# A hybrid attention and mLSTM trunk: the mixer's transposes move from TensorE to transposing DMAs, all but two, and the second token tile's output takes its mLSTM half first

## The chip, the cores and the metric

The kernel runs on one core of a Trainium2 chip. The metric is the device time of one execution in microseconds (us). The time before the change is the median of three runs, 963.02 us (962.27 to 963.16).

## The reference

The input x has 256 tokens of 1024 channels (batch 1). There are two layers. Each adds to x a half-step SwiGLU network, a mixer, and another half-step SwiGLU network; every branch has an RMS norm ahead of it and one behind it. The mixer, cut to what matters:

```python
proj = h @ w_in                                  # 1024 -> 3080 columns
da_q, da_k, da_v, ml_qk, ml_v, ml_o, ml_g = split(proj)
# differential attention, 4 heads of 2 x 64, causal in chunks of 64 tokens
q = rope(da_q) * 64 ** -0.5; k = rope(da_k)
p = softmax(where(mask, q @ k.T, -inf))          # two maps per head
y_da = rmsnorm((p[0] - lam * p[1]) @ v) * (1 - lam_init)
# mLSTM, 4 heads, chunked recurrence over the tokens
q, k = split(silu(causal_conv(ml_qk)))           # 4 taps over the tokens
y_ml = sigmoid(ml_o) * rmsnorm(numerator / denominator)
out = concat([y_da, y_ml]) @ w_out               # 1024 -> 1024
```

Everything is in 32-bit floats.

## The kernel before

The 256 tokens are two tiles of 128 tokens, numbered 0 and 1 here and in the code (`t`). Weights are streamed from memory in pieces of 1 MB (`wr`), by SyncE's DMA queue and into three buffers. ScalarE rounds each half piece to the reduced 32-bit format (`wh`, L288), VectorE takes the difference (`wl`, L289), and TensorE multiplies in three passes: activation high by weight high, high by low, low by high (`mm3`, L401, L402, L403). In the three passes the activation is the stationary side and 512 weight columns move.

A layer is a list of such products. In the mixer, `traverse` lays out the products of the six projections in 56 or so steps, one step being the three passes for 128 input channels of one token tile. The order of projections is: the mLSTM's q and k (whose convolution follows), the attention's Q and K with rope, the mLSTM's values, the attention's values, and the mLSTM's output gate. All other work of the mixer (gates, convolution, scores, softmax, numerators) is cut into stages, which `stages` lists; the table `AT` (L40) says ahead of which step each stage is written. So TensorE's stream alternates projection steps with short groups of the stages' own products. Which instruction goes when on each engine is decided by the scheduler of the framework, which keeps the written order on TensorE nearly as it is and may move instructions on the others; `high_priority` blocks pull an evacuation forward. Every engine then runs its own list in order.

PSUM has two banks for projections (tag `pin`), two for transposes (`ptr`) and four for the rest (`bk`). A projection's bank is free again once its evacuation has read it: `nat` for the convolution input (`conv_input`), `rv` for Q and K (`rope`), `vx` and `vd` for the values, `so` (a Tanh) for the output gate. With two banks, a projection waits for the evacuation of the one but last.

The places where the mixer turns a 128x512 tile of tokens by channels into channels by tokens are these, each by four TensorE transposes into one `ptr` bank and one ScalarE copy out of it:

- the convolution input `nat`, both tiles (`conv_input_t`, L898), into the padded buffer `xpad`;
- the rope's result `ra`, Q and K for both tiles (`roped`, L1067), into `qkT`;
- the combined attention weights `p`, once for tile 0 and twice for tile 1 (`combine`, L1110), into `aT`; here VectorE first forms p[0] + c * p[1] in place (L1122);
- the attention output `y` and the gated mLSTM output `so` of both tiles (`attended`, `outputs_ml`), followed by `hilo`, which scales them and splits them into a high and a low part (L884, L885).

The feed-forward networks already turn their hidden activations in another way (`ffn_planes`, L530). ScalarE copies the tile, read as 16-bit words, into two planes of low and high halves (L535); a transposing DMA on SyncE's queue turns the planes (L537); VectorE joins the halves to 32-bit words again (L539).

At the end of a mixer, `outp(t, part, hf)` multiplies one half of the output vector (`part` 0 is attention, 1 is mLSTM) of tile `t` into 512 output columns `hf`, four steps of three passes each.

## Time and profile before

| | before |
|---|---|
| median of three runs | 963.02 us (962.27 to 963.16) |
| the profiled execution | 962.02 us |
| its span in the trace | 960.2 us |
| granted TensorE clock | 0.999 |
| busy: TensorE matmul, its weight load | 952.8 us, 788.9 us |
| busy: VectorE, ScalarE, GpSimd | 638.7 us, 571.2 us, 29.5 us |
| DMA traffic | 189.32 MB, mean 197 GB/s |

The profile is of one execution. Its own time of 962.02 us is 1.0 us below the median of the runs; the span is the part that the trace covers, from the first recorded instruction to the last. PE is TensorE's matmul stream and PEld its weight load, which overlaps it; DVE is VectorE, ACT ScalarE, POOL GpSimd, and SP is SyncE, whose queue issues nearly all DMAs. L numbers are lines of the kernel before. The two mixers lie at about 191 to 290 us and 664 to 763 us of the span; the feed-forward networks fill the rest.

### The profile page before, as it was taken

Reading aid. Unit: us, or ns where it says so; the run is one execution under the profiler, and the core shown is the slowest. Engines: PE = TensorE matmul, PEld = TensorE weight load, DVE = VectorE, ACT = ScalarE, POOL = GpSimd, SP = SyncE. Lnnn points to the kernel's source line nnn. Section 1 sums busy time; section 2 is a strip of 40 time slices with the busy share of each in tenths; the row PEclk is TensorE's granted clock in tenths of the full one; section 3 lists DMA queues with packets and bytes.
Section 4 is the critical chain, followed back from the end, with each engine's and each line's share of the span. In section 5 each row is a group of like instructions: output and inputs, shape, how many; then the busy total and the mean of one; then the engine's idle time right before and its main releaser. Section 6 shows DMA issues by size and latency. Waiting matters only on the chain.

```text
span 960.2 us, 12037 instructions
## 1 busy us (share of the span) xinstructions
PE 952.8 (99%) x4523; PEld 788.9 (82%) x4523; DVE 638.7 (67%) x945; ACT 571.2 (59%) x937; POOL 29.5 (3%) x55
## 2 busy tenths in 40 slices
PE   9999999999999999999999999999999999999997
PEld 7888888888888888888888888888888888888885
DVE  6765655689867766555687555566988676755553
ACT  8755554577856655454476555555778466555542
POOL 2000000000010000000000000000001000000000
PEclk9999999999999999999999999999999999999999
DMA  8996656236352975676458666653454257765621
GB/s 317 328 288 202 225 193 219 105 132 241 116 192 91 299 245 193 218 247 176 154 189 283 206 225 208 196 187 128 172 202 174 90 182 256 272 205 192 225 72 44
DMA packets 69879, 189.32 MB, mean 197 GB/s; under 512 B 45274, under 2 KB 46426, under 8 KB 49086
## 3 DMA queue, kind: packets, MB, share of 16 engines
q1 hardware_dynamic: 69246, 187.95, 58.0%
q8 instruction: 35, 0.57, 0.2%
q10 hardware_dynamic: 576, 0.61, 0.2%
q14 instruction: 22, 0.18, 0.1%
HBM read 177.01 MB, written 1.05 MB: 185 GB/s over the span
## 4 chain that ended last, share of the span: by engine, by line
PE 97%; DVE 1%; DMA 1%; ACT 0%; issue 0%; POOLq 0%; DVEq 0%; ACTq 0%
PE pin L401 13%; PE pin L402 13%; PE pin L403 13%; PE bk L401 10%; PE bk L402 10%; PE bk L403 10%; PE ptr L402 6%; PE ptr L403 6%; PE ptr L401 6%; PE pin L610 1%; PE ptr L610 1%; PE ptr L879 1%; PE ptr L427 1%; DMA wr<-in_w_dram 1%; PE bk L1094 1%; PE ptr L615 1%
## 5 line engine op out<-in xcount | busy, mean ns | idle before, releaser
L289 DVE TENSOR_TENSOR wl<-wr,wh 128x1024 fp32r<-128x1024 f32 x324 | 389.2, 1221 | 180.4 <-ACT wh L288 174.4
L288 ACT ACTIVATE wh<-wr 128x1024 fp32r<-128x1024 f32 x324 | 333.9, 1055 | 171.2 <-DMA wr<-in_w_dram 44.1
L401 PE MATMUL pin<-wh,both 128*128 128x512 f32 x560 | 221.2, 396 | 0.0
L403 PE MATMUL pin<-wh,both 128*128 128x512 f32 x560 | 218.3, 390 | 0.0
L402 PE MATMUL pin<-wl,both 128*128 128x512 f32 x560 | 218.2, 390 | 0.0
L401 PE MATMUL bk<-wh,hh 128*128 128x512 f32 x352 | 137.4, 390 | 0.1
L402 PE MATMUL bk<-wl,hh 128*128 128x512 f32 x352 | 137.0, 389 | 0.0
L403 PE MATMUL bk<-wh,hl 128*128 128x512 f32 x352 | 136.9, 389 | 0.0
L403 PEld LDWEIGHTS pin<-wh,both 128*128 128x128 f32 x560 | 105.1, 188 | 22.3
L401 PEld LDWEIGHTS pin<-wh,both 128*128 128x128 f32 x560 | 105.3, 188 | 22.0 <-issue 0.7
L402 PEld LDWEIGHTS pin<-wl,both 128*128 128x128 f32 x560 | 105.3, 188 | 20.6
L403 PE MATMUL ptr<-wh,both 128*128 128x512 f32 x256 | 99.4, 389 | 0.0
L402 PE MATMUL ptr<-wl,both 128*128 128x512 f32 x256 | 99.4, 389 | 0.0
L401 PE MATMUL ptr<-wh,both 128*128 128x512 f32 x256 | 98.9, 389 | 0.0
L401 PEld LDWEIGHTS bk<-wh,hh 128*128 128x128 f32 x352 | 66.1, 188 | 14.0 <-ACT hh L550 0.5
L403 PEld LDWEIGHTS bk<-wh,hl 128*128 128x128 f32 x352 | 66.1, 188 | 13.7
L402 PEld LDWEIGHTS bk<-wl,hh 128*128 128x128 f32 x352 | 66.1, 188 | 13.5
L539 DVE COPY hT<-turned 128x1024 uint16<-128x1024 uint16 x40 | 30.3, 757 | 41.9 <-DMA turned<-planes 41.5
L401 PEld LDWEIGHTS ptr<-wh,both 128*128 128x128 f32 x256 | 48.1, 188 | 10.0
L402 PEld LDWEIGHTS ptr<-wl,both 128*128 128x128 f32 x256 | 48.1, 188 | 10.0
L550 ACT ACTIVATE hh<-hT 128x256 fp32r<-128x256 f32 x80 | 28.9, 409 | 46.0 <-DVE hT L539 46.0
L403 PEld LDWEIGHTS ptr<-wh,both 128*128 128x128 f32 x256 | 48.1, 188 | 9.9
(210 smaller groups left out, 891.9 us busy)
## 6 DMA issues: line engine op xcount, KB each, us to landing
wr<-in_w_dram SPq DMA_DIRECT2D x162, 1024.0 KB, 5.2
gpost<-in_gpost_dram SPq DMA_DIRECT2D x6, 512.0 KB, 6.3
wr<-in_w_dram SPq DMA_DIRECT2D x2, 512.0 KB, 6.1
wr<-in_w_dram SPq DMA_DIRECT2D x3, 256.0 KB, 4.3
x<-in_x_dram SPq DMA_DIRECT2D x3, 256.0 KB, 4.4
turned<-planes SPq DMA_TRANSPOSE x40, 4.4
out_dram<-x SPq DMA_DIRECT2D x2, 256.0 KB, 2.1
x<-in_x_dram SPq DMA_DIRECT2D x2, 128.0 KB, 3.0
```

Of the source, the lines that this page charges most:

```text
L288: ia = nc.scalar.activation(hi, raw[:, j], AF.Copy)
L289: iv = nc.vector.tensor_tensor(lo, raw[:, j], hi.bitcast(F32), op=ALU.subtract)
L401: mm(ps, xh, wh, start=start, stop=False)
L402: mm(ps, xh, wl, start=False, stop=False)
L403: mm(ps, xl, wh, start=False, stop=stop)
L427: nc.tensor.transpose(ptr[:, k, :], x[:, (4 * hf + k) * P:(4 * hf + k + 1) * P], self.ident)
L539: nc.vector.tensor_copy(hT.rearrange("p b n -> p (b n)").bitcast(U16).rearrange("p (n u) -> p u n", u=2), turned.rearrange("p (u b) n -> p ...
L550: self.nc.scalar.activation(hh, h, AF.Copy)
L610: self.nc.tensor.matmul(b, self.cols(w[kh], k)[0][:, c], both[kh][:, k].rearrange("p i t -> p (i t)"), start=kh == 0 and k == 0, stop=Fals ...
L615: self.nc.tensor.matmul(b[:, 0:NT * P], self.cols(w[kh], k)[1][:, c], both[kh][:, k, 0:NT].rearrange("p i t -> p (i t)"), start=False, sto ...
L879: self.T(ptr[:, b, :], a[:, b * P:(b + 1) * P], self.tr.ident)
L1094: self.mm(pcs[c][:, h, :], self.qkT[0][rows, h0 + h, t * P:(t + 1) * P], self.qkT[1][rows, h0 + h, 0:nk], start=True, stop=True)
```

## The change

The mixer's turns go the way of the feed-forward networks' hidden activations: planes on ScalarE, a transposing DMA on SyncE's queue, a joining copy on VectorE. Only `y` and `so` of tile 0 keep TensorE's transposes. Per mixer that is eleven groups of four transposes gone from TensorE, and eleven times planes, DMA and joining copy added. Nine of ScalarE's evacuations go with them; for `y` and `so` of tile 1 `hilo` stays and reads the joined tile. The issue of the DMA moves to where the tile is made (`turn` in `conv_input`, `rope`, `combine`, `attend`, `output_gate`), and the joining copy stands where the transposes were; for the attention weights that is a stage of its own (`weights`). The factor 1/8 of Q goes into the scale of its evacuation (`rhalf`). `combine` writes its sums into a tile of its own, `pc`. The two stages `attended` are written earlier or outside `stages`, the table `AT` has a value for every new stage, and the output projection of tile 1 takes `part` 1 first.

```diff
+    def turn(self, v):
+        planes = self.t2("planes", (P, 2, 512), U16)
+        self.nc.scalar.activation(planes, v.bitcast(U16).rearrange("p (n u) -> p u n", u=2), AF.Copy)
+        turned = self.t2("turned", (P, 8, P), U16)
+        self.nc.sync.dma_start_transpose(turned, planes.rearrange("p u n -> p (u n)"))
+        return turned
+
+    def joined(self, out, turned):
+        self.nc.vector.tensor_copy(out.bitcast(U16).rearrange("p b (n u) -> p u b n", u=2),
+                                   turned.rearrange("p (u b c) n -> p u b (c n)", u=2, b=out.shape[1]))
...
         outp(0, 1, 0)
         m.outputs_ml(1)
+        m.attended(1)
         outp(0, 1, 1)
         yield "done", po[0], gpost
+        outp(1, 1, 0)
+        outp(1, 1, 1)
+        yield "next"
         outp(1, 0, 0)
         outp(1, 0, 1)
-        yield "next"
-        outp(1, 1, 0)
-        outp(1, 1, 1)
         yield "done", po[1], gpost
...
-        self.nat = nat
+        self.nat.append(tr.turn(nat))
 
     def conv_input_t(self, t):
-        self.act(self.xpad[:, :, 3 + t * P:3 + (t + 1) * P], self.transposed(self.nat), AF.Copy)
+        self.tr.joined(self.xpad[:, :, 3 + t * P:3 + (t + 1) * P], self.nat[t])
...
-        self.rot.append(a)
+        self.rot.append(tr.turn(a))
...
-        self.act(self.qkT[i][:, :, t * P:(t + 1) * P], self.transposed(self.rot[2 * i + t]), AF.Copy, scale=scale)
+        self.tr.joined(self.qkT[i][:, :, t * P:(t + 1) * P], self.rot[2 * i + t])
...
-        ptr = tr.bank_tr((P, t + 1, nh, P))
+        pc = tr.t2("pc", (P, t + 1, nh, P))
         for h in range(nh):
-            p = self.p[t, h0][h]
-            self.stt(p[:, 0, :], p[:, 1, :], c1[:, h:h + 1], p[:, 0, :], op0=ALU.mult, op1=ALU.add)
-            for kt in range(t + 1):
-                self.T(ptr[:, kt, h, :], p[:, 0, kt * P:(kt + 1) * P], tr.ident)
-        self.act(aT[:, :, hs, :], ptr, AF.Copy)
+            p = self.p[t, h0][h].rearrange("p c (a b) -> p c a b", b=P)
+            self.stt(pc[:, :, h, :], p[:, 1], c1[:, h:h + 1], p[:, 0], op0=ALU.mult, op1=ALU.add)
+        self.flat[t, h0] = aT[:, :, hs, :], tr.turn(pc.rearrange("p a h b -> p (a h b)"))
+
+    def weights(self, t, h0):
+        out, turned = self.flat[t, h0]
+        self.tr.joined(out.rearrange("p a h b -> p a (h b)"), turned)
...
-        self.y[t] = y
+        y = y.rearrange("p h e -> p (h e)")
+        self.y[t] = tr.turn(y) if t else y
...
-        y = self.transposed(self.y[t].rearrange("p h e -> p (h e)"))
+        y = self.whole(self.y[t]) if t else self.transposed(self.y[t])
...
-        self.so.append(so)
+        so = so.rearrange("p h e -> p (h e)")
+        self.so.append(tr.turn(so) if t else so)
```

The scheduler's order shows three places in the first mixer. In these rows line numbers are those of the kernel listed; in the kernel after the change, planes are L544, the joining copy L550, the rope's evacuation `rv` L1071 and the gate's exponentials still L266.

VectorE, at the start of the mixer, before: `gs` to `lg` are the gate's small steps, `g_591` holds the gate rows that TensorE transposes next, and `wl` are weight splits.

```order
L433 TENSOR_TENSOR both_1700<-xg_1829,both_1700 128x4x128
L289 TENSOR_TENSOR wl_0_1863<-wr_1861,wh_0_1864 128x1024
L289 TENSOR_TENSOR wl_1_1867<-wr_1861,wh_1_1868 128x1024
L940 TENSOR_REDUCE gs_1896<-bk_1895 128x16
...
L949 SCALAR_TENSOR_TENSOR lg_1917<-gn_1897 128x8
L755 TENSOR_SCALAR c_neglam<-c_neglam 128x1
L289 TENSOR_TENSOR wl_0_1982<-wr_1980,wh_0_1983 128x1024
L957 SCALAR_TENSOR_TENSOR g_591<-gn_1897,lg_1917 128x4x4 x2
L289 TENSOR_TENSOR wl_1_1992<-wr_1980,wh_1_1993 128x1024
L973 SCALAR_TENSOR_TENSOR gt_2011<-c_scan,bk_1931 100x256
```

The same place after; `xpad` is the padded convolution input of tile 0.

```order
L433 TENSOR_TENSOR both_1700<-xg_1833,both_1700 128x4x128
L550 COPY xpad<-turned_1817 128x2x4x128
L289 TENSOR_TENSOR wl_0_1861<-wr_1859,wh_0_1862 128x1024
L289 TENSOR_TENSOR wl_1_1865<-wr_1859,wh_1_1866 128x1024
L950 TENSOR_REDUCE gs_1894<-bk_1893 128x16
...
L959 SCALAR_TENSOR_TENSOR lg_1915<-gn_1895 128x8
L289 TENSOR_TENSOR wl_0_1991<-wr_1989,wh_0_1992 128x1024
L289 TENSOR_TENSOR wl_1_2001<-wr_1989,wh_1_2002 128x1024
L967 SCALAR_TENSOR_TENSOR g_591<-gn_1895,lg_1915 128x4x4 x2
L983 SCALAR_TENSOR_TENSOR gt_2026<-c_scan,bk_1929 100x256
```

The joining copy into `xpad` now stands ahead of the splits `wl_0_1861` and `wl_1_1865`, and both splits of the next piece stand ahead of the gate rows, where one did.

ScalarE, around Q's tile 1, before: `rv_1996` is the evacuation of Q's tile 1 from bank `pin_1961`, `eE` are the gate's two exponentials, `conv` the first tap of the convolution in four blocks.

```order
L288 ACTIVATE wh_1_2132<-wr_2113 128x1024
L1057 ACTIVATE rv_1996<-pin_1961,rs_204_1840 128x512
L288 ACTIVATE wh_0_2182<-wr_2179 128x1024
L899 ACTIVATE xpad<-ptr_2032 128x4x128
L266 ACTIVATE eE_2050<-bk_2047 128x512
L907 ACTIVATE conv_2038<-xpad,c_568 128x256 x4
L266 ACTIVATE eE_2055<-bk_2052 128x512
L260 ACT_TABLE_LOAD
L1071 ACTIVATE qkT_2057<-ptr_2058 128x4x128
```

The same place after; `planes_1966` is for the rope's result of Q's tile 0, and `rv_2005` is the evacuation of Q's tile 1.

```order
L288 ACTIVATE wh_0_2190<-wr_2187 128x1024
L917 ACTIVATE conv_2048<-xpad,c_568 128x256 x4
L544 ACTIVATE planes_1966<-ra_1957 128x1024
L266 ACTIVATE eE_2060<-bk_2057 128x512
L266 ACTIVATE eE_2065<-bk_2062 128x512
L260 ACT_TABLE_LOAD
L1071 ACTIVATE rv_2005<-pin_1970,rhalf_2008 128x512
```

Q's evacuation went from ahead of the convolution, the exponentials and the table load to behind all of them. On TensorE the second exponential's input `bk_2062` is made directly ahead of `pin_2067`, K's tile 1, which takes the bank of `pin_1970`:

```order
L1008 MATMUL bk_2057<-md,ul 128x512
L1009 MATMUL bk_2057<-c_mask,c_identr 128x512
L1008 MATMUL bk_2062<-md,ul 128x512
L1009 MATMUL bk_2062<-c_mask,c_identr 128x512
L401 MATMUL pin_2067<-wh_0_1992,both_1690 128x512
L402 MATMUL pin_2067<-wl_0_1991,both_1690 128x512
```

Before, two groups of transposes stood around these four products; no other product moved there.

VectorE, around the attention weights, before: `p` are the softmax maps of tile 0 being combined, `bk_2357` and the next are the scores of tile 1, whose masked part is set (L1097) and whose maxima are then taken (L1098, `mx`).

```order
L1122 SCALAR_TENSOR_TENSOR p_2272<-p_2272,c_262_2338 128x128 x2
L1122 SCALAR_TENSOR_TENSOR p_2273<-p_2273,c_262_2338 128x128 x2
L289 TENSOR_TENSOR wl_1_2558<-wr_2500,wh_1_2559 128x1024
L289 TENSOR_TENSOR wl_0_2644<-wr_2642,wh_0_2645 128x1024
L1097 MEMSET bk_2357 64x2x64
L1098 TENSOR_REDUCE mx_2355<-bk_2357 128x2
L1097 MEMSET bk_2358 64x2x64
L1098 TENSOR_REDUCE mx_2355<-bk_2358 128x2
```

The same place after; `turned_2346` comes from the transposing DMA of tile 0's combined weights `pc_2339`.

```order
L1136 SCALAR_TENSOR_TENSOR pc_2339<-p_2275,c_270_2336 128x128 x2
L1136 SCALAR_TENSOR_TENSOR pc_2339<-p_2276,c_270_2336 128x128 x2
L289 TENSOR_TENSOR wl_1_2529<-wr_2496,wh_1_2530 128x1024
L289 TENSOR_TENSOR wl_0_2643<-wr_2641,wh_0_2644 128x1024
L1111 MEMSET bk_2354 64x2x64
L1111 MEMSET bk_2355 64x2x64
L550 COPY aT_259_2258<-turned_2346 128x2x512
L1112 TENSOR_REDUCE mx_2352<-bk_2354 128x2
```

The joining copy of tile 0's weights now stands between the masks and the maxima of tile 1.

More of the change, by code (lines that the diff above doesn't have):

```diff
@@ L39 @@
 AHEAD = 2
-AT = (0, 2, 6, 6, 7, 22, 24, 24, 24, 24, 36, 40, 24, 46, 34, 50, 43, 52, 52, 57, 61, 60, 61, 67, 67, 69, 71, 78, 74, 74, 78, 84)
+AT = (0, 2, 6, 6, 7, 10, 22, 24, 24, 24, 24, 36, 40, 28, 46, 34, 50, 46, 52, 52, 57, 61, 60, 61, 67, 67, 69, 71, 78, 72, 74, 78, 80, 82, 83)
 FIRST = """W6 V3 T000 T001 A000 A001 B000 B001 W1 V1 T002 T003 H00 L00 A002 A003 B002 B003 W1 V1 M000 H01 L01
@@ L148 @@
     TAGS = {"kwn": ("kwn", 1), "aT0": ("aT0", 1), "aT1": ("aT1", 1)}
-    for _n in ("nat", "ra", "rb", "rv", "tmp", "y", "so", "xg", "h", "planes", "turned", "hT"):
+    for _n in ("nat", "ra", "rb", "rv", "tmp", "y", "so", "xg", "h", "planes", "turned", "hT", "pc"):
         TAGS[_n] = ("ev", 5)
@@ L530, in ffn_planes @@
     def ffn_planes(self, h):
-        nc = self.nc
-        planes = self.t2("planes", (P, 2, 512), U16)
-        nc.scalar.activation(planes, h.rearrange("p t j -> p (t j)").bitcast(U16).rearrange("p (n u) -> p u n", u=2), AF.Copy)
-        turned = self.t2("turned", (P, 8, P), U16)
-        nc.sync.dma_start_transpose(turned, planes.rearrange("p u n -> p (u n)"))
         hT = self.t2("hT", (P, 4, P))
-        nc.vector.tensor_copy(hT.rearrange("p b n -> p (b n)").bitcast(U16).rearrange("p (n u) -> p u n", u=2),
-                              turned.rearrange("p (u b) n -> p u (b n)", u=2))
+        self.joined(hT, self.turn(h.rearrange("p t j -> p (t j)")))
         ops = [self.ffn_operand() for _ in range(NT)]
@@ L731, in outp @@
                 self.mm3(po[t][hf], yh[:, k, :], yl[:, k, :], *self.cols(ws[2 * part + k // 2], 2 * (k % 2) + hf),
-                         start=part == 0 and k == 0, stop=part == 1 and k == 3)
+                         start=part == t and k == 0, stop=part != t and k == 3)
         outp(0, 0, 0)
@@ L765, in __init__ @@
         self.conved = None
-        self.rot, self.qkT, self.so, self.p = [], [], [], {}
+        self.nat, self.rot, self.qkT, self.so, self.p, self.flat = [], [], [], [], {}, {}
         self.aT, self.lsum, self.hn, self.y = [None] * NT, [None] * NT, [None] * NT, [None] * NT
@@ L836, in stages @@
             self.gate_rows,
+            lambda: self.conv_input_t(0),
             self.gate_chain,
@@ L843, in stages @@
             lambda: self.conv((0, 1)),
-            lambda: self.roped(0, 0, 0.125),
+            lambda: self.roped(0, 0),
             self.conv_silu,
-            lambda: self.roped(0, 1, 0.125),
+            lambda: self.roped(0, 1),
             self.weighted_qk,
-            lambda: self.roped(1, 0, 1.0),
+            lambda: self.roped(1, 0),
             lambda: self.scores(0, 0),
             self.intra_weights,
-            lambda: self.roped(1, 1, 1.0),
+            lambda: self.roped(1, 1),
             lambda: self.scores(1, 0),
@@ L859, in stages @@
             lambda: self.normed_ml(1),
+            lambda: self.weights(0, 0),
             lambda: self.attend(0),
+            lambda: self.attended(0),
+            lambda: self.weights(1, 0),
+            lambda: self.weights(1, 2),
             lambda: self.attend(1),
-            lambda: self.attended(0),
-            lambda: self.attended(1),
         ))
@@ L1055, in rope @@
         v8, a8, b8 = (i.rearrange("p (g d) -> p g d", g=8) for i in (v, a, b))
+        scale = self.r[t]
+        if len(self.rot) < NT:
+            scale = tr.small("rhalf", (P, 1))
+            self.ts(scale, self.r[t], 0.125, None, op0=ALU.mult)
         with tr.tc.high_priority():
-            self.rv = self.act(v, pin, AF.Copy, scale=self.r[t])
+            self.rv = self.act(v, pin, AF.Copy, scale=scale)
             i = tt(a8, v8, tr.rope[:, 0, t, :].unsqueeze(1).broadcast_to([P, 8, 64]), op=ALU.mult)
@@ L1064, in rope, with roped @@
             self.turned = tt(a, a, b, op=ALU.add)
-        self.rot.append(a)
-    def roped(self, i, t, scale):
+        self.rot.append(tr.turn(a))
+    def roped(self, i, t):
         if t == 0:
             self.qkT.append(self.tr.t4("qkT", (P, 4, S)))
-        self.act(self.qkT[i][:, :, t * P:(t + 1) * P], self.transposed(self.rot[2 * i + t]), AF.Copy, scale=scale)
+        self.tr.joined(self.qkT[i][:, :, t * P:(t + 1) * P], self.rot[2 * i + t])
     def values_da(self, pin, t):
@@ L1142, in attend, with whole @@
         self.tt(y, po, sc.unsqueeze(2).broadcast_to([P, 4, P]), op=ALU.mult)
-        self.y[t] = y
+        y = y.rearrange("p h e -> p (h e)")
+        self.y[t] = tr.turn(y) if t else y
+    def whole(self, turned):
+        out = self.tr.t2("hT", (P, 4, P))
+        self.tr.joined(out, turned)
+        return out
     def attended(self, t):
-        y = self.transposed(self.y[t].rearrange("p h e -> p (h e)"))
+        y = self.whole(self.y[t]) if t else self.transposed(self.y[t])
         self.yT[t][0] = self.hilo(y, self.tr.gda[:, self.l:self.l + 1], 0, t)
@@ L1213, in outputs_ml @@
     def outputs_ml(self, t):
-        y = self.transposed(self.so[t].rearrange("p h e -> p (h e)"))
+        y = self.whole(self.so[t]) if t else self.transposed(self.so[t])
         self.yT[t][1] = self.hilo(y, self.tr.gml[:, self.l:self.l + 1], 1, t)
```

1 line of the change is left out of this document (removed).

## The prediction

> **What bounds the kernel now.** I read the page first: the busy shares, then the chain that ended last.
>
> ```profile
> PE 952.8 (99%) x4523; PEld 788.9 (82%) x4523; DVE 638.7 (67%) x945; ACT 571.2 (59%) x937; POOL 29.5 (3%) x55
> PE 97%; DVE 1%; DMA 1%; ACT 0%; issue 0%; POOLq 0%; DVEq 0%; ACTq 0%
> ```
>
> TensorE is busy all the time and the chain runs on it. So a TensorE instruction that disappears is worth its full time, and any wait that makes TensorE stand still costs its full time. Other engines cost nothing until TensorE needs something from them. The averages hide the stage that the change touches, so next I read windows over the two mixers, and one inside the first.
>
> ```profile
> 191.00:286.00 95.00, 95.00 (x535) 78.61 (x534) 78.42 (x151) 69.75 (x152) 6.22 (x9) 1.00 0.47 172
> 664.00:759.00 95.00, 95.00 (x535) 78.65 (x534) 78.27 (x148) 70.02 (x152) 7.33 (x9) 1.00 0.47 172
> 220.00:225.00 5.00, 5.00 (x24) 4.14 (x23) 5.00 (x12) 4.97 (x8) 0.00 (x0) 1.00 0.77 299
> ```
>
> The columns after the length are busy time of PE, PEld, DVE, ACT and POOL, the granted clock, the DMA share and GB/s. The mixers are alike, so one is worked out and doubled. In a mixer VectorE is busy for 78.4 of 95 us (67% over the whole span) and in 220 to 225 us both VectorE and ScalarE are full. What the change hands to them lands where they have least to spare.
>
> **What is removed.** On the chain of waits the groups of four transposes stand as follows (start, us):
>
> ```profile
> 217.62 0.44 PE ptr L879 x4
> 248.23 0.62 PE ptr L1124 x4
> 256.38 0.58 PE ptr L1124 x4
> 260.65 0.44 PE ptr L1124 x4
> ```
>
> Per mixer the code drops eleven groups: two of the convolution input, four after the rope, three of the attention weights, one each of the token-1 halves y and so. Eight at 0.44 and 0.62 + 0.58 + 0.44 make 5.16 us; for two mixers 10.3 us. All of it is on the path, so that is the most that the change can gain. The scheduled order shows that TensorE's other work stays the same, but for the attention product of token 1, which moves 24 rows later.
>
> **What is added.** Per mixer eleven plane copies on ScalarE, eleven transposing DMAs in SyncE's queue, eleven joining copies on VectorE. The FFN already does all three, so their prices stand in the trace:
>
> ```profile
> L535 ACT ACTIVATE planes<-h 128x1024 uint16<-128x1024 uint16 x40 | 42.1, 1052 | 8.6 <-DVE h L528 8.4
> L539 DVE COPY hT<-turned 128x1024 uint16<-128x1024 uint16 x40 | 30.3, 757 | 41.9 <-DMA turned<-planes 41.5
> L1125 ACT ACTIVATE aT<-ptr 128x512 f32<-128x512 f32 x6 | 3.5, 589 | 0.0
> DMA to landing us min/median/max: 2.7/4.4/8.9
> ```
>
> A turn by TensorE costs 0.44 us and an evacuation of 0.59 on ScalarE. By DMA it costs 1.05 + 2.7 (the fastest; 4.4 is the median) + 0.76 = 4.5 us at least, passed through three queues. VectorE gets 11 x 0.76 = 8.3 us more per mixer, ScalarE 11 x 1.05 less nine evacuations of 0.6, so 6.2 us. VectorE then has 86.7 us of work in about 90: nearly full, not yet the bound. What suffers first could be the weight halves (L289). One that by the order is first read by K's products for token 0:
>
> ```profile
> 203.36 1.22 DVE L289 TENSOR_TENSOR wl<-wr,wh 128x1024 fp32r<-128x1024 f32 x1 [0.24 <-ACT wh L288]
> 214.72 0.39 PE L401 MATMUL pin<-wh,both 128*128 128x512 f32 x1
> ```
>
> It is done at 204.6 and read at 214.7: 10 us ahead. The 8.3 us come spread over the mixer, and TensorE's own delay gives the splits as much time again, so I cost the splits at nothing; with that cover gone it is the third rival.
>
> The Trainium skill, VectorE: DVE Perf Modes, section Rules for kernel authors, advises TensorE for a 128x128 transpose if PSUM can be the target, which speaks against this change; its section on the three transpose paths prices the DMA's at 1309 ns for one block of 16-bit values. By that figure the eight blocks of one plane tile would take 10.5 us (an estimate), and the sum below would grow by up to 4 x 7.8 us a mixer; the trace has 2.7 us, which I use.
>
> **Gate rows.** A joining copy for the convolution input now stands on VectorE ahead of two pairs of weight splits, and the gate's rows (before at 204.50) behind both pairs.
>
> ```profile
> 194.05 12.20 SPq L282 DMA_DIRECT2D wr<-in_w_dram  x3
> 198.85 2.36 DVE L289 TENSOR_TENSOR wl<-wr,wh 128x1024 fp32r<-128x1024 f32 x2 [0.25 <-ACT wh L288]
> 204.50 0.25 DVE L957 SCALAR_TENSOR_TENSOR g<-gn,lg 128x16 f32<-128x16 f32 x2
> 205.39 0.60 PE L967 MATMUL bk<-c,g 128*100 128x128 f32 x4
> ```
>
> The turn is queued behind the weight load of 194.05; I put its landing at 199.75. Copy 0.76, two splits 2.36, small steps 1.0, two splits 2.36: the rows come at about 206.3. TensorE is there 0.36 earlier than before, at 204.8. Stall about 1.45 us, from 0 (an earlier landing, splits in between) to 3 (landing at the 4.4 median).
>
> **Rope of Q's second token.** Before, the evacuation rv ran as soon as its products were done. Now it is last on ScalarE behind four convolution steps, a plane copy, both gate exponentials and the table load. The next projection reuses the PSUM bank that rv empties, so TensorE waits for rv.
>
> ```profile
> 214.92 0.69 ACT L1057 ACTIVATE rv<-pin,rs 128x512 f32<-128x512 f32 x1 [0.30 <-PE pin L403]
> 219.06 2.07 ACT L907 ACTIVATE conv<-xpad,c 128x256 f32<-128x256 f32 x4
> 221.03 0.58 ACT L266 ACTIVATE eE<-bk 128x512 f32<-128x512 f32 x1
> 221.63 1.28 ACT L260 ACT_TABLE_LOAD   x1
> 218.59 0.40 PE L999 MATMUL bk<-c_mask,c_identr 128*128 128x512 f32 x1
> 219.18 0.48 PE L401 MATMUL pin<-wh,both 128*128 128x512 f32 x1
> ```
>
> The second exponential reads the product that TensorE makes directly before the blocked projection, so part of this wait can't be hidden whatever the load: 0.4 (product) + 0.58 + 1.28 + 0.69 = 2.85 us after removing what overlaps. By the queue I get more, since the convolution steps wait for VectorE's second copy into the padded input, and VectorE is full here:
>
> ```profile
> 210.00:215.00 5.00, 5.00 (x24) 4.14 (x23) 4.82 (x11) 3.83 (x7) 0.00 (x0) 1.00 0.02 7
> 215.00:220.00 5.00, 5.00 (x28) 4.17 (x27) 4.94 (x7) 3.48 (x6) 0.00 (x0) 1.00 0.59 225
> ```
>
> With the gate work 1.45 later in that queue I put the copy's end at 217.75; convolution to 219.8, planes 220.8, two exponentials 221.9, table 223.2, rv 223.9. TensorE, 1.45 late and 1.24 early, would come at about 219.5. Stall 4.4 us (2.85 to 5.5, a copy 1 us later). To here, 5.85 of stalls less 1.24 of transposes: +4.6.
>
> The Trainium skill, ScalarE: Activation LUTs, section What ACT_TABLE_LOAD costs, adds a drain of about 1380 ns to the load's 1283. The trace shows the load at 1.28 us and the next instruction starting at its end; by the page this stall would be 1.4 us longer.
>
> **K's second token to the first scores.** The same rv step, one token later, waits behind one plane copy: a stall of 1.0, less two groups of 0.44: +0.1 (-0.9 to +1.5).
>
> **Scores to the last projection.** Here a whole chain becomes serial: token 0's exponentials, combination, planes, DMA, joining copy, which stands ahead of token 1's maxima on VectorE; these release token 1's exponentials, and behind them stands the evacuation vd that frees the next projection's bank.
>
> ```profile
> 239.98 1.16 PE L1094 MATMUL bk<-qkT,qkT 64*128 64x128 f32 x16
> 246.34 0.40 ACT L266 ACTIVATE p<-bk,mx 128x128 f32<-128x128 f32 x1
> 247.32 1.14 DVE L1122 SCALAR_TENSOR_TENSOR p<-p,c 128x128 f32<-128x128 f32 x4
> 250.95 0.69 DVE L1098 TENSOR_REDUCE mx<-bk 128x2 f32<-128x512 f32 x1
> 251.73 0.47 ACT L266 ACTIVATE p<-bk,mx 128x256 f32<-128x256 f32 x1 [1.87 <-DVE mx L1098]
> 260.80 0.67 ACT L1077 ACTIVATE vd<-pin,rs 128x512 f32<-128x512 f32 x1
> 261.63 0.39 PE L401 MATMUL pin<-wh,both 128*128 128x512 f32 x1
> ```
>
> Count from the scores' start, 239.98. Before: exponentials of token 0 done at 6.8, of token 1 begun at 11.75, vd done at 21.5, its user at 21.65. So TensorE had 0.16 us to spare. After: 6.8 + 1.7 (combination) + 1.05 + 2.7 + 0.76 + 0.7 = 13.8 with hand-overs; from there to vd 9.74 as before, + 1.05 (planes of token 1) - 0.59 (evacuation gone) + 0.2: vd at 24.2. TensorE, without 2.08 us of transposes, would be there at 19.57. Stall 4.8 us with hand-overs. Behind it two smaller ones: the numerators of token 1 wait for hn, which follows another joining copy on VectorE (from vd on a split 0.95, two squares 0.5, planes, DMA, copy and hn 1.3 make 7.1 to 7.3 us, against 5.3 of TensorE's own work: 1.8); the transpose of y for token 0, 0.3. Together 6.9 - 2.08 = +4.8 (+3 to +6.5; the upper end is a DMA at 4.4).
>
> **Output.** Token 1's mLSTM half comes first and its turn is the last link.
>
> ```profile
> 276.29 0.69 DVE L1190 SCALAR_TENSOR_TENSOR so<-so,hn 128x512 f32<-128x512 f32 x1
> 276.45 0.68 ACT L884 ACTIVATE both<-ptr,c 128x512 fp32r<-128x512 f32 x1
> 277.93 0.60 PE L879 MATMUL ptr<-c,so 128*128 128x128 f32 x4
> 283.87 0.60 PE L879 MATMUL ptr<-c,so 128*128 128x128 f32 x4
> ```
>
> The Tanh now follows the evacuation of token 0's so (3.6 us after the last projection) and the planes of y. From there 0.7 + 1.05 + 0.7 + 0.7 + 1.05 + 2.7 + 0.76 + 0.7: ready at about 12.2, needed at 11.4, the 48 products of token 0 (0.23 us each) and one transpose group. That token 1 takes this half first costs nothing by itself: it is the same 48 products in another order. Its y half is read 24 products later, behind cover of 5 us. Stall 1.0 (0 to 4) less 0.88 saved: +0.1 (-0.9 to +2.5).
>
> **Sum.** 4.6 + 0.1 + 4.8 + 0.1 = 9.6 us per mixer, 19.3 for both. The profiled execution took 962.02 us, so it becomes 981.3; the median of the runs is 1.0 us above that: 982. With every low end a mixer gets 1.6 - 0.9 + 3.0 - 0.9 = +2.8, with every high end 7.3 + 1.5 + 6.5 + 2.5 = +17.8.
>
> **Rivals.**
> First, everything hides but the structural part of rv (the faster side). Place: vd and the maxima. If the joining copy doesn't hold the maxima back, or exponentials begin sooner than my count, token 1's chain keeps the 4.8 us and only 2.85 us per mixer is paid: 962.0 - 10.3 + 5.7 = 957.4, about 958 by the median. It decides when stalls beside rv's stay under 2.3 us a mixer. For it: ScalarE sat idle for 1.87 us just ahead of token 1's first exponential (the row of 251.73), so some of the chain has slack. Against: vd had 0.16 us to spare. Chance 0.10.
> Second, half of my stalls at rows and vd: about 5 us a mixer against 5.16: no change. Chance 0.05.
> Third, VectorE or SyncE's queue becomes the bound: transposes stuck behind 1 MB loads at 4.4 us or more, weight halves late as well. Four DMAs on the path, each 1.7 longer, add 6.8 a mixer: 962.0 + 2 x 16.4 + 1.0 = 996. It decides when VectorE's work exceeds the mixer's own time, or the median landing replaces the fastest. For it: 86.7 of 90 us. Against: in the mixers the DMA share is 0.47. Chance 0.13.
>
> **How the numbers follow.** The forecast has 0.72. A measurement can tell about 0.2%, 1.9 us. Faster 0.10, same 0.05, slower 0.85. The range drops the first two rivals (0.15) and the upper part of the third (0.05): from 966, just below all low ends (962.0 + 5.6 + 1.0 = 968.6), to 993, +15 a mixer. All high ends at once I count with the third.
>
> **What would show it.** In the profile after, TensorE's idle time per mixer should be about 14 us, in four places: before the gate rows, before K's second token with ScalarE's rv as releaser (4.4), before the last projection with vd (4.8), before token 1's output. VectorE near 87 us per mixer. It is wrong if rv is not the releaser, if vd's wait is under 2 us, or if the FFN stages change by more than a microsecond.

## The result and the profile after

The changed kernel takes 996.41 us (median of four runs, 995.01 to 997.17) against 962.64 us before in the same comparison: a ratio of 1.035 (95% interval 1.033 to 1.037). The forecast was 982, from 966 to 993: the sign was right, the size was not. The loss is 33.8 us where 19.3 were forecast. The profiled execution took 995.01 us, 33.0 more than the one before; its span is 993.2 us. One execution of those in the table further down is left out of its ratio: conv_behind's second took 1368.67 us at a granted clock of 0.654, its other five 964.75 to 965.75.

The page of the kernel after, its busy shares and the head of the chain that ended last:

```profile
PE 957.2 (96%) x4435; PEld 787.3 (79%) x4435; DVE 653.8 (66%) x971; ACT 584.7 (59%) x941; POOL 28.1 (3%) x55
PE 83%; DMA 6%; DVE 5%; ACT 4%; issue 2%; POOL 0%; SPq 0%; POOLq 0%; ACTq 0%; DVEq 0%
```

The chain now leaves TensorE for 17% of the span, most of it for transposing DMAs, VectorE and ScalarE. What TensorE waited for in the kernel after, largest first (total us, times, longest us):

```profile
PE pin L401 <- ACT rv L1071: 13.0, 4, 4.1
PE pin L401 <- ACT vd L1091: 5.5, 2, 2.7
PE ptr L889 <- DVE y L1158: 2.7, 2, 1.4
PE bk L977 <- DVE g L967: 2.3, 2, 1.3
PE bk L1194 <- DVE hn L1233: 1.7, 1, 1.7
PE bk L1194 <- ACT p L266: 1.4, 2, 0.7
```

Adding every gap of more than 0.15 us in the two mixers gives 14.5 us in the first and 13.4 in the second, 27.9 together; the forecast's stalls were 14.75 a mixer, 29.5. So the waits are as large as forecast. They do not make up the loss: 27.9 less the 10.3 us of removed transposes is 17.6, and 33.0 were lost. Most of the other 15.4 us stands in a row that looks harmless: PE is busy for 957.2 us, more than the 952.8 before, although 88 transposes are gone. TensorE itself was slower. And it was slower in the mixers alone: matched product by product, TensorE falls back by 19.8 us in the first mixer and 13.4 in the second, and by nothing in the feed-forward networks.

The windows show where. Kernel after, first mixer, columns as before (the third number from the end is the granted clock):

```profile
215.00:220.00 5.00, 3.94 (x18) 2.89 (x16) 4.91 (x7) 4.03 (x8) 0.00 (x0) 1.00 0.54 174
220.00:225.00 5.00, 1.93 (x5) 1.54 (x6) 5.00 (x11) 2.99 (x5) 0.00 (x0) 0.71 0.82 231
225.00:230.00 5.00, 5.00 (x15) 3.91 (x14) 3.13 (x9) 3.50 (x4) 0.00 (x0) 0.61 1.05 174
```

From 225 to 230 us TensorE is busy all the time and issues 15 products, where such a window before had 24. The same place as a timeline of TensorE, kernel after:

```profile
218.54 0.40 PE L1009 MATMUL bk<-c_mask,c_identr 128*128 128x512 f32 x1
223.07 0.79 PE L401 MATMUL pin<-wh,both 128*128 128x512 f32 x1 [4.14 <-ACT rv L1071]
223.66 0.63 PE L402 MATMUL pin<-wl,both 128*128 128x512 f32 x1
224.09 0.63 PE L403 MATMUL pin<-wh,both 128*128 128x512 f32 x1
...
228.36 0.63 PE L401 MATMUL pin<-wh,both 128*128 128x512 f32 x1
228.78 0.46 PE L402 MATMUL pin<-wl,both 128*128 128x512 f32 x1
229.08 0.40 PE L403 MATMUL pin<-wh,both 128*128 128x512 f32 x1
```

After the wait of 4.14 us, 13 products follow each other at 0.43 us instead of 0.23, then the pace is back. The granted clock in the windows falls with them. Such a stretch stands behind six places of this execution: 13, 7, 6 and 9 products in the first mixer, 7 and 6 in the second. Five stand behind one wait of 2.29 to 4.14 us. The one of 9 products stands behind two shorter waits, with 1.75 us of work between them:

```profile
282.30 0.91 PE L1194 MATMUL bk<-vx,wt 128*128 128x129 f32 x6 [1.67 <-DVE hn L1233]
...
285.34 1.11 PE L889 MATMUL ptr<-c,y 128*128 128x128 f32 x4 [1.29 <-DVE y L1158]
286.10 0.78 PE L401 MATMUL pin<-wh,both 128*128 128x512 f32 x1
286.68 0.63 PE L402 MATMUL pin<-wl,both 128*128 128x512 f32 x1
```

The forecast priced a wait at its length; it can cost up to 2.8 us on top. The 48 slow products at 0.2 us each make 9.6 of the 15.4 us. An estimate for some 3 us more: a gap is counted from a product's modelled end, 0.40 us after its start, while in an unbroken stream the next starts after 0.23, so each of the 17 gaps hides 0.17 us. The rest, about 3 us, stays open.

### The profile page after: what moved, and what is told of

Read it like the earlier page. It is cut to its first block, busy times and chain, and to the rows that moved or that the text cites. A ratio compares the mean times of both kernels' runs of the same rounds, so it can differ in the third digit from the quotient of the medians.

```text
span 993.2 us, 11947 instructions
## 1 busy us (share of the span) xinstructions
PE 957.2 (96%) x4435; PEld 787.3 (79%) x4435; DVE 653.8 (66%) x971; ACT 584.7 (59%) x941; POOL 28.1 (3%) x55
## 3 DMA queue, kind: packets, MB, share of 16 engines
HBM read 177.01 MB, written 1.05 MB: 179 GB/s over the span
## 4 chain that ended last, share of the span: by engine, by line
PE 83%; DMA 6%; DVE 5%; ACT 4%; issue 2%; POOL 0%; SPq 0%; POOLq 0%; ACTq 0%; DVEq 0%
PE pin L401 10%; PE pin L402 10%; PE pin L403 10%; PE bk L403 9%; PE bk L401 9%; PE bk L402 9%; PE ptr L403 6%; PE ptr L402 6%; PE ptr L401 6%; DMA turned<-planes 5%; DVE wl L289 2%; PE pin L617 1%; PE ptr L617 1%; ACT planes L544 1%; PE ptr L427 1%
## 5 line engine op out<-in xcount | busy, mean ns | idle before, releaser
L401 PE MATMUL pin<-wh,both 128*128 128x512 f32 x560 | 225.9, 404 | 18.5 <-ACT rv L1071 13.0
L402 PE MATMUL pin<-wl,both 128*128 128x512 f32 x560 | 222.0, 396 | 0.0
L403 PE MATMUL pin<-wh,both 128*128 128x512 f32 x560 | 221.7, 396 | 0.0
L401 PEld LDWEIGHTS pin<-wh,both 128*128 128x128 f32 x560 | 107.6, 192 | 44.6 <-ACT rv L1071 14.7
L403 PEld LDWEIGHTS pin<-wh,both 128*128 128x128 f32 x560 | 107.4, 192 | 23.2
L402 PEld LDWEIGHTS pin<-wl,both 128*128 128x128 f32 x560 | 107.9, 193 | 21.5
L550 DVE COPY hT<-turned 128x1024 uint16<-128x1024 uint16 x44 | 33.0, 756 | 51.3 <-DMA turned<-planes 51.2
```

Source lines behind the costliest of these rows:

```text
L401: mm(ps, xh, wh, start=start, stop=False)
L402: mm(ps, xh, wl, start=False, stop=False)
L403: mm(ps, xl, wh, start=False, stop=stop)
L550: self.nc.vector.tensor_copy(out.bitcast(U16).rearrange("p b (n u) -> p u b n", u=2), turned.rearrange("p (u b c) n -> p u b (c n)", u=2, ...
```

## The experiments

Theory: the stalls were forecast rightly, and each stall over some 2 us costs TensorE's clock for a few microseconds behind it. Rivals: the slow products come from something else in the mixers (DMA traffic, full engines); or the losses belong to VectorE and SyncE's queue, and a wait removed at one place returns at the next. All times are compared with the kernel before on the same chip. The clock in the last column is the granted one of the profiled execution.

| run | median us | ratio to before (95%) | clock |
|---|---|---|---|
| the change | 996.41 | 1.035 (1.033 to 1.037) | 0.985 |
| warm | 999.43 | 1.038 (1.037 to 1.040) | 0.986 |
| warm_all | 990.91 | 1.030 (1.029 to 1.032) | 0.998 |
| ev6 | 993.39 | 1.032 (1.030 to 1.033) | 0.985 |
| rv_own | 991.18 | 1.030 (1.029 to 1.031) | 0.988 |
| rope_pe | 981.39 | 1.019 (1.016 to 1.022) | 0.990 |
| comb_pe | 979.41 | 1.018 (1.017 to 1.020) | 0.993 |
| both_pe | 969.35 | 1.007 (1.005 to 1.009) | 0.996 |
| only_conv | 967.71 | 1.006 (1.005 to 1.008) | 0.998 |
| conv_behind | 965.40 | 1.003 (1.002 to 1.005) | 0.999 |
| only_out | 965.51 | 1.004 (1.002 to 1.005) | 0.999 |
| only_y1 | 961.01 | 0.9987 (0.9979 to 0.9996) | 0.998 |
| ladder | 1078.32 | 1.121 (1.119 to 1.123) | 0.956 |

### warm: fill the three long waits

```diff
+KEEP = {24: 16, 40: 9, 72: 10}
...
+            if s in KEEP:
+                tr.warm(KEEP[s], tr=True)
             if s < len(steps):
                 steps[s]()
```

> The changed kernel with 16, 9 and 10 empty 512-column products on TensorE (bf16, into a transpose bank that nothing reads) ahead of the three products that wait longest in each mixer: K's tile 1 (waits rv, 4.1 us idle), the mLSTM values' tile 1 (waits rv, 2.3), the output gate's tile 1 (waits vd, 2.7). They take about 0.22 us each, so 3.5, 2.0 and 2.2 us, less than the idle time they stand in; no data wait is shortened. Theory (the stalls are about as forecast, and the other half of the loss is TensorE's clock, which is granted at about half after a stall): the products behind these places run at 0.23 us instead of 0.43, the granted clock rises from 0.985 to 0.995 or more, and the time falls by 9 to 14 us to about 985. Rival (the slow products come from the DMA engines, whose share is over 1.0 in the same windows, or from another engine's traffic): they stay at 0.43 us and the time stays at 996 or grows by up to 2.

TensorE at the place shown above, in the run warm (lines here are one to three higher):

```profile
218.96 3.44 PE L391 MATMUL ptr<-const-bfloat16-1.0 128*128 128x512 bf16 x15
223.02 0.51 PE L402 MATMUL pin<-wh,both 128*128 128x512 f32 x1 [0.61 <-ACT rv L1074]
223.37 0.40 PE L403 MATMUL pin<-wl,both 128*128 128x512 f32 x1
223.60 0.40 PE L404 MATMUL pin<-wh,both 128*128 128x512 f32 x1
```

The product that waits for rv starts at 223.02, as before at 223.07, with the same data waits, and the products behind it run at 0.23 us. So with TensorE kept busy, the same wait for data has no slow stretch behind it. The traffic has changed only in part: in the two windows from 220 us the DMA share is 0.83 and 0.71, where the kernel after has 0.82 and 1.05. What speaks against the DMAs is a window of the kernel before, with as high a share and 25 products at full pace (run warm first, then the kernel before):

```profile
220.00:225.00 5.00, 4.39 (x21) 2.51 (x19) 5.00 (x11) 3.21 (x6) 0.00 (x0) 1.00 0.83 241
225.00:230.00 5.00, 5.00 (x24) 4.13 (x23) 4.12 (x11) 4.34 (x5) 0.00 (x0) 1.00 0.71 164
```

```profile
10.00:15.00 5.00, 5.00 (x25) 4.19 (x24) 4.58 (x13) 5.00 (x14) 0.04 (x1) 1.00 1.04 435
```

But the time did not fall: 999.43. The two gaps of 1.40 and 1.71 us around token 1's numerators and y now made slow stretches in both mixers (12 and 10 products), and two gaps grew and drew 8 and 13 slow products: 2.49 us at the gate rows of the second mixer and 2.96 before tile 1's output of the first. The forecast of this run's time was wrong, because it left these places out.

### warm_all: fill every wait

Beside the edit of warm, ahead of tile 1's output and in `gate_rows`, `attended` and `normed_ml`:

```diff
+        self.warm(6, tr=True)
         outp(1, 1, 0)
...
         tr, T, g2 = self.tr, self.T, self.tr.g2
+        tr.warm(4, tr=True)
...
     def attended(self, t):
+        if not t:
+            self.tr.warm(6, tr=True)
...
+        if t:
+            tr.warm(5, tr=True)
         num = self.numerators(t)
```

> The changed kernel with empty 512-column products on TensorE ahead of every place that waited over 0.6 us in it or in the run with three fillings: 4 before the gate rows, 16, 9 and 10 as there, 5 before token 1's numerators, 6 before the transposes of y, 6 before tile 1's output: 56 of 0.22 us per mixer, 12.4 us. No data wait is shortened, and some fillings overshoot. Theory (slow products come from TensorE's own idle time alone): hardly any slow product is left, the granted clock is 0.997 or more, and the time is 962 - 8.4 (transposes) + 30 to 36 (waits and fillings) = 984 to 990, below the changed kernel's 996 although TensorE has more to do. Rival (the three fillings only moved the slow stretches, which come of themselves): clock at 0.985 and 996 or more.

Measured 990.91 us with the clock at 0.998, and no slow stretch in either mixer. TensorE has 25.0 us of fillings and 9.9 us of gaps over 0.15 us, 34.9 together against the change's 27.9, and is still 5.5 us faster than it. Against the span before (960.2): 25.0 + 9.9 - 10.3 = 24.6, measured 29.1 (span 989.3). The remainder falls from 15.4 us to 4.5. So some 10 to 11 us of the loss are TensorE's slower pace, and idle time is what brings it. The time is 1 us over the expected range; the gap of 1.94 us at rv of K's tile 1 was under-filled.

### ladder: the disputed cost by itself

```diff
+        first = self.nc.tensor.matmul(bank[:, 0:P], one, self.probe, start=True, stop=True)
+        self.after(first, [self.last_mm])
+        for _ in range(n):
+            self.nc.gpsimd.memset(self.probe, 0.0)
+        self.gate = self.nc.tensor.matmul(bank[:, 0:P], one, self.probe, start=True, stop=True)
```

> The kernel before, with 24 waits put into the feed-forward networks, six in each of the four, one per chunk: a small empty product on TensorE, then 5, 8, 11, 14, 17 or 20 fills of a small tile on GpSimd, then a second small product that reads the tile; TensorE's later products are held behind it. Nothing of the mixers is touched. It measures the disputed cost by itself: products that are slow behind a wait. Theory (a wait of TensorE over some 2 us costs half the clock for a few us, wherever it stands): behind the short waits (about 1 to 1.5 us) products run at 0.23 us, behind the long ones (over 2.5) at 0.43 for 1.5 to 6 us, behind those between it is one or the other; each long wait costs 1 to 3 us more than its length. Rival (slow products belong to the mixers' transposing DMAs and full engines): all products stay at 0.23 us and the time grows by the waits' own sum.

Two of the waits in TensorE's timeline, the run ladder; the first product behind each wait, and where the pace changes:

```profile
69.76 0.22 PE L602 MATMUL pin<-c_probe,const-bfloat16-1.0 128*128 128x128 bf16 x1 [1.37 <-POOL c_probe L601]
69.79 0.48 PE L403 MATMUL ptr<-wh,both 128*128 128x512 f32 x1
70.11 0.39 PE L406 MATMUL ptr<-wl,both 128*128 128x512 f32 x1
...
88.66 0.22 PE L602 MATMUL ptr<-c_probe,const-bfloat16-1.0 128*128 128x128 bf16 x1 [2.21 <-POOL c_probe L601]
...
89.47 0.40 PE L403 MATMUL pin<-wh,both 128*128 128x512 f32 x1
89.70 0.59 PE L406 MATMUL pin<-wl,both 128*128 128x512 f32 x1
90.09 0.63 PE L407 MATMUL pin<-wh,both 128*128 128x512 f32 x1
...
93.08 0.43 PE L403 MATMUL pin<-wh,both 128*128 128x512 f32 x1
```

Behind 1.37 us nothing happens. Behind 2.21 us the products first run at full pace for 1 us, then 7 run at 0.43, from 89.70 to 93.08: 3.4 us. Over the whole run, by the length of the wait:

| wait us | slow products behind it |
|---|---|
| 0.25 to 1.18 (five, broken up by other work) | none |
| 1.37, 1.43 (two) | none |
| 1.82 (1.18 us idle stand 2 us ahead of it) | 7 |
| 2.21 (three), 2.51, 2.94, 3.00 (two) | 7 each |
| 3.72, 3.78 (two) | 11 to 13 |
| 4.57 (four) | 7 to 12 |
| 5.29, 5.35 (two) | 9 or 10 |

The counts hold to within one, since a stretch begins and ends with products between the two paces. These are in the feed-forward networks, far from the change. The rival is out: the price belongs to the wait. In round figures a wait of 2.2 us or more costs 1.4 to 2.8 us more than it lasts, and beyond 3.7 us how much more does not grow with its length. Where the price begins is a region and not a line: waits of 1.67 us at y in ev6 and 1.71 in rope_pe have 8 slow products behind them, while 1.94 us in both_pe and 2.43 in the kernel after have none.

The Trainium skill, TensorE: Matmul & The Clock Gate, Part 1, describes this as a gate on TensorE's clock that watches activity in free-running windows of about 3.4 us and halves the clock after an idle one. The 3.4 us stretch at half pace and the delayed start at 89.70 agree. The Trainium skill, same page, section Why this matters for your kernels, asks for no idle gaps of more than about 3 us; here 2.21 us was enough three times out of three, less than one such window, and the measurement decides.

### ev6 and rv_own: why rv is late

```diff
-        TAGS[_n] = ("ev", 5)
+        TAGS[_n] = ("ev", 6)
```

> The changed kernel with six buffers in place of five for the tiles nat, ra, rb, rv, planes, turned, hT and the like; the room comes from unused filler and one buffer of C. The order on every engine is the same, row for row; only what a buffer's reuse waits for moves. With five, rv of K's tile 1 takes the buffer of the planes of Q's tile 1 and so waits for their transposing DMA; with six it doesn't. Theory (that reuse is the 2.3 us wait which the forecast put at 1.0): the second wait on rv falls below 0.5 us in both mixers, the first (4.1) stays; with the slow products behind it the time falls by 5 to 7 us to about 990. Rival (rv is late because its own queue on ScalarE is): the wait stays over 2 us and the time within 2 us of 996.

ScalarE in the kernel after shows rv of K's tile 1 released by a DMA: the planes of Q's tile 1 sit in the buffer that it is to take, and their transposing DMA had been issued behind a 1 MB load.

```profile
232.22 0.33 SPq L282 DMA_DIRECT2D wr<-in_w_dram  x1
232.66 1.23 SPq L546 DMA_TRANSPOSE turned<-planes  x1
238.55 0.69 ACT L1071 ACTIVATE rv<-pin,rs 128x512 f32<-128x512 f32 x1 [2.06 <-DMA turned<-planes]
```

Issued at 232.66, landed at 238.5: 5.9 us where 2.7 was reckoned. With six buffers, TensorE's waits are:

```profile
PE pin L401 <- ACT rv L1071: 8.3, 2, 4.1
PE pin L401 <- ACT vd L1091: 5.5, 2, 2.8
PE ptr L889 <- DVE y L1158: 3.2, 2, 1.7
PE bk L977 <- DVE g L967: 1.8, 2, 1.0
PE bk L1108 <- DVE qd L1038: 1.6, 1, 1.6
```

The second wait on rv is gone in both mixers: four waits have become two. The time falls by only 3 us of the 5 to 7 expected: in the second mixer a new wait of 1.6 us appears at the scores, with 4 slow products behind it, and y's wait of 1.67 us now draws 8. The trace has 50 slow products, where the kernel after has 48. In rv_own, rv has one buffer of its own:

```diff
-    TAGS = {"kwn": ("kwn", 1),
+    TAGS = {"rv": ("rv", 1), "kwn": ("kwn", 1),
```

> The changed kernel with a buffer of its own for the rope's rv, which leaves the shared five to the rest (room from unused filler and one buffer of C). In the scheduled order rv of Q's tile 1 now stands ahead of the convolution again, as in the kernel before; all turns stay with DMAs. Theory (both waits on rv come from the shared buffers: the first through the order that they force, the second through the wait for a DMA): both go in both mixers, 13.0 us, with the 6 us of slow products behind them: 996 - 19 = about 977, what is left being vd, the numerators, y and the gate rows. Rival (time removed early is waited for later, as six buffers showed in part): the waits at vd and the scores grow and the time stays above 985.

TensorE's wait in rv_own, and then VectorE and ScalarE ahead of the product that waits (the two lines L1072 and L1077 at 234 us read the rv before):

```profile
PE pin L401 <- ACT rv L1071: 11.1, 2, 5.6
```

```profile
230.56 0.73 DVE L550 COPY qkT<-turned 128x1024 uint16<-128x1024 uint16 x1
...
231.57 2.36 DVE L289 TENSOR_TENSOR wl<-wr,wh 128x1024 fp32r<-128x1024 f32 x2
233.84 0.69 DVE L1072 TENSOR_TENSOR ra<-rv,c 128x512 f32<-128x512 f32 x1
234.44 0.76 DVE L1077 TENSOR_TENSOR rb<-rv,c 128x256 f32<-128x256 f32 x2
```

```profile
235.29 0.69 ACT L1071 ACTIVATE rv<-pin,rs 128x512 f32<-128x512 f32 x1 [2.55 <-DVE rb L1077]
```

The wait of 4.1 us at Q's tile 1 is gone: it was not bound to the gate's exponential, as the forecast had it, but to the place in ScalarE's order that the shared buffers gave to rv. The wait at K's tile 1 is 5.6 us instead: with a single buffer, rv waits until VectorE has read the rv before it, and those reads stand behind a joining copy and two weight splits. So the rival holds for this pair: 991.18, not 977. Which of the two, buffers or VectorE's queue, would still hold rv with two own buffers was not tried.

### rope_pe, comb_pe, both_pe: undo one part

```diff
-        self.rot.append(tr.turn(a))
+        self.rot.append(a)
...
-        self.tr.joined(self.qkT[i][:, :, t * P:(t + 1) * P], self.rot[2 * i + t])
+        self.act(self.qkT[i][:, :, t * P:(t + 1) * P], self.transposed(self.rot[2 * i + t]), AF.Copy)
```

> The changed kernel with the rope's four turns per mixer back on TensorE, all else as changed. Theory: both waits on rv go (4.1 + 2.3 us in the first mixer, 4.1 + 2.4 in the second, 13.0 together) and the slow products behind them (about 6 us), and eight transpose groups come back (8 x 0.44 = 3.5): 996 - 19 + 3.5 = about 981. Rival (VectorE's and SyncE's queues are what is short, and a wait removed early is paid later): the chain at the attention weights keeps its length and TensorE waits there for what it no longer waits for at rv, so the time stays above 990.

981.39 us, as expected; the waits on rv are gone. That the number came out is partly luck: the gate rows of the second mixer wait 2.76 us instead of 1.33, with 8 slow products, which was not expected. The wait on vd is 3.2 us in both mixers, half a microsecond more than after the change, and stays the largest. comb_pe puts the attention weights back:

```diff
-        pc = tr.t2("pc", (P, t + 1, nh, P))
+        ptr = tr.bank_tr((P, t + 1, nh, P))
...
+            for kt in range(t + 1):
+                self.T(ptr[:, kt, h, :], p[:, 0, kt * P:(kt + 1) * P], tr.ident)
+        self.act(aT[:, :, hs, :], ptr, AF.Copy)
```

> The changed kernel with the three turns of the attention weights per mixer back on TensorE, all else as changed. Theory: the waits on vd go (2.7 each), those on token 1's numerators too (0.7 each and 1.7), with the slow products behind them (3 to 6 us); the transposes come back with 2 x 1.64 = 3.3 us: 996 - 13 + 3 = 985 to 988. The rv waits stay at 4.1 and 2.3. Rival (vd is late because VectorE is full, not because of the serial chain through the DMA): vd still waits over 2 us and the time stays above 992.

979.41 us, better than expected: no wait on vd or on the numerators, and rv of K's tile 1 waits 1.2 and 0.95 us instead of 2.3, where three DMAs fewer pass through the shared buffers and the queue. VectorE is relieved of only three copies of 0.76 us a mixer, so the serial chain through the DMA is the likelier cause of vd's wait than a full VectorE; the run takes both away and does not part them. both_pe has both edits:

> The changed kernel with the turns of the rope and of the attention weights back on TensorE; the convolution input (2 per mixer) and y and so of tile 1 stay with DMAs, and the output of tile 1 still takes its mLSTM half first. Theory: stalls of about 1.0 to 1.3 us at the gate rows and 0.7 at the output are left, 1.8 per mixer, against 1.6 of transposes saved, with no stall over 2 us and so no slow clock: 962.6, within 2 us either way. Rival (what costs is any transposing DMA in the mixer, by SyncE's queue and the weight loads): 965 to 972.

969.35 us, where 962.6 was expected: the rival's range. What remains in its trace are gaps of 0.89 and 2.76 us at the gate rows, 1.94 + 0.37 and 0.83 + 0.36 before tile 1's output, 0.5 us at y, and one slow stretch. Two parts that looked free are not.

### only_conv, conv_behind, only_out, only_y1: one part alone

only_conv is the kernel before with `conv_input`, `conv_input_t` and the latter's place among the stages as in the change:

```diff
-        self.nat = nat
+        self.nat.append(tr.turn(nat))
...
-        self.act(self.xpad[:, :, 3 + t * P:3 + (t + 1) * P], self.transposed(self.nat), AF.Copy)
+        self.tr.joined(self.xpad[:, :, 3 + t * P:3 + (t + 1) * P], self.nat[t])
```

> The kernel before with one part of the change alone: the convolution input's two turns per mixer by DMA. Theory: 1.6 us of transposes saved in both mixers together, the gate rows wait 0.9 to 2.8 us a mixer, as in the run that kept this part and the output's, with slow products behind a wait over 2: 964 to 966 against 962.2. Rival (that wait came from the output part of the layer before or from the weight loads it displaced): no wait there, 960.6.

```profile
PE bk L979 <- DVE g L969: 3.8, 2, 2.9
PE ptr L891 <- DVE ra L1076: 1.7, 1, 1.7
```

967.71 us, over the expected 964 to 966. The gate rows wait 0.94 and 2.90 us, the second with 7 slow products, and in the first mixer the rope's result is late too. conv_behind ties the copy behind the gate rows:

```diff
-        self.tr.joined(self.xpad[:, :, 3 + t * P:3 + (t + 1) * P], self.nat[t])
+        i = self.tr.joined(self.xpad[:, :, 3 + t * P:3 + (t + 1) * P], self.nat[t])
+        if t == 0:
+            self.tr.after(i, [self.gl])
```

> The kernel before with the convolution input's two turns per mixer by DMA, as in the run with that part alone, and the first joining copy tied in order behind the gate rows on VectorE. Theory (that copy's place ahead of the gate rows made the waits of 0.9 and 2.9 us and the slow products): those waits go, 962.0 - 1.4 for four transpose groups a layer pair, plus up to 1.8 where the rope's result waited on VectorE: 961 to 963. Rival (VectorE's 1.5 us more work is itself what the gate rows and the rope wait for): 965 to 968 as without the tie.

```profile
PE ptr L891 <- DVE ra L1078: 3.5, 2, 1.8
PE bk L981 <- DVE g L971: 0.9, 2, 0.4
```

The gate rows' waits fall to 0.44 us each, so the copy's place made most of them. The rope's result is now 1.75 us late in both mixers and not only in the first; that VectorE has no room for the two copies there is argued and not shown. 965.40, still slower than before, at the rival's lower end. only_out is the kernel before with `y` and `so` of tile 1 by DMA and the swapped halves:

```diff
+        self.y[t] = tr.turn(y) if t else y
...
+        self.so.append(tr.turn(so) if t else so)
...
+        outp(1, 1, 0)
+        outp(1, 1, 1)
+        yield "next"
         outp(1, 0, 0)
         outp(1, 0, 1)
```

> The kernel before with the other small part alone: y and so of tile 1 turned by DMA and the output of tile 1 taking its mLSTM half first; the attention product of tile 1 stays where it was. Theory: 1.76 us of transposes saved in both mixers, waits before tile 1's output of 2.3 and 1.2 us (as in the run that kept both parts): 962.2 + 3.5 - 1.8 = 964. Rival (with the attention product early and ScalarE relieved, so's chain hides): 960.4, faster than before.

965.51 us. The trace has gaps of 0.92 + 0.36 and 0.87 + 0.36 us before tile 1's output, 2.5 together against 1.76 saved; its execution took 963.55 us. The eleven runs spread from 962.61 to 969.44. The five over 966 us have a granted clock of 0.996 or 0.997, five of the six others 0.998 or 0.999, which fits slow products behind a wait, but what the longer ones had is in no trace; that stays open. only_y1 turns y of tile 1 alone and leaves the halves' order:

```diff
         m.outputs_ml(1)
+        m.attended(1)
         outp(0, 1, 1)
...
+        self.y[t] = tr.turn(y) if t else y
```

> The kernel before with one turn per mixer by DMA: the attention output y of tile 1, whose product comes over 5 us after it. The order of the output's halves stays. Theory (a turn by DMA pays where its 4.5 us chain has cover and nothing urgent stands behind it in a queue): no wait, two transpose groups saved, 962.0 - 0.7 = 961.3. Rival (planes and copy delay token 1's so or the weight load behind the DMA): 962.5 to 964.

961.01 us, the one version that is faster than before, by 0.13% (0.04 to 0.21%). In its trace TensorE has no gap in either mixer that the profile shows.

## Why the prediction was wrong, point by point

- **What bounds the kernel**: right. TensorE is the bound, and every wait was paid in full. "Any wait that makes TensorE stand still costs its full time" was too mild: this is the step that failed. A wait from some 2 us on costs its time and, mostly, 1.2 to 2.8 us of half-paced products. The sum itself held four waits over 4 us, at rv of Q and at vd in both mixers, and added nothing for them; in the trace after these four and two other places drew the price. The ladder shows the price alone, warm_all removes about 11 of the 15.4 us.
- **What is removed**, 10.3 us: no run contradicts it.
- **Gate rows**, 1.45: measured 0.95 and 1.33, for the reason given; conv_behind, where 0.44 is left, shows it. The forecast's 204.8 counts from the product ahead of the gate rows; from its own row of 205.39 it is 205.0, and the stall 1.3.
- **Rope of Q's second token**, 4.4: measured 4.14 and 4.13. The row and the size were right, the "part that can't be hidden" was not: rv_own has no wait there with all turns by DMA. In the kernel after, rv started at 222.33, at the end of the table load (221.04 and 1.28 us), with no further delay.
- **K's second token**, 1.0: measured 2.29 and 2.43. Mis-sized and for the wrong reason. The forecast saw a plane copy ahead of rv; the wait is the reuse of a buffer that a DMA of 5.9 us still reads. ev6 shows it.
- **Scores to the last projection**, 4.8 at vd, 1.8 at hn, 0.3 at y: measured 2.73 and 2.75 at vd; 1.67 and none at hn; 1.29 and 1.43 at y; and 0.67 and 0.68 at token 0's numerators, which the forecast did not have. In sum 6.4 and 4.9 for 6.9. vd ended 23.9 us after the scores began, 24.2 in the forecast; TensorE got there 1.6 us later than the count, 0.7 of it by the wait at the numerators, the rest not shown, and so waited less.
- **Output**, 1.0: measured 0.75 and 0.68. The forecast's own figures, ready at 12.2 and needed at 11.4, make 0.8.
- **The rivals**: everything hidden, no. The third rival's 996 is the time that was measured, but by luck, since its mechanism is not what happened: the gaps were no longer than forecast, VectorE is busy for 66% of the span and the fastest landing and the median of the transposing DMAs (2.7 and 4.3 us) are as before. Two landings, 9.6 us for Q's tile 0 and 5.9 for its tile 1, were of its kind. VectorE's work a mixer came out at 86 us, as reckoned (87), and the networks' time did not change.
- **The range**: all low and high ends were taken over lengths of waits. No row of the trace before shows a product behind a wait: TensorE has no gap over 0.15 us between its first product and its last, and the clock stood at 1.00 in every window read. But the half pace itself is in that trace. The kernel begins with six empty 512-column products (L390), which start at 0.76, 1.14, 1.56, 1.99, 2.42 and 2.85 us, 0.4 us apart; in warm_all and warm such products take about 0.22. A TensorE that comes out of idleness was slow there too, and a bound for the price could have been taken from it.

## What to carry to other kernels

A stall of a matmul engine that was never idle before has a second price, which the length of the stall does not hold: count each forecast wait over 2 us with up to 2.8 us more, and distrust those from 1.6 us on. Several short waits are cheaper than a long one only where they stand apart: 1.67 and 1.29 us close together drew the price here. The runs fit the view that a step moved to a DMA pays only where its whole chain of 4.5 us has cover and where nothing urgent stands behind it, neither in the engines' queues nor in the buffers that the DMA still reads. Of the parts tried here one, y of tile 1, gained, and by 0.13%; most turns were tried in groups, and so of tile 1 never without y.

## What the runs showed of the hardware

- TensorE's pace halves (0.43 us for 0.23 per 128x512 product) after idle times from about 2 us (2.21 us in the ladder three times of three, 1.67 once in ev6, not 2.43 in the kernel after), mostly for 6 to 13 products; the fall can come a microsecond after the work has resumed (88.66 to 89.70 in the ladder).
- Empty products keep the pace: 56 of them a mixer made a kernel with 34.9 us of fillings and gaps 5.5 us faster than one with 27.9 us of gaps.
- A transposing DMA of one tile took 2.7 us at the least, and 5.9 and 9.6 us where a 1 MB load had been issued 0.4 us ahead of it on the same queue (at 232.22 and 220.33). The kernel after, from issue to landing over all 62 of them:

```profile
DMA to landing us min/median/max: 2.7/4.3/9.7
```
